# Fixed places on ScalarE for scaled output copies and rounding of operand sums, and a second pass that begins with one block product alone

## The chip, the cores and the metric

The kernel runs on one core of a Trainium2 chip. The metric is the device time of one execution in microseconds; the time of a kernel is the median of its runs.

## The reference

One layer of a hybrid decoder trunk for a sequence of 1024 tokens and 1024 channels, in float32: two token mixers in parallel, then an MLP.

```
h = rms_norm(x); xa, ga, q, f, v, g, m_a, m_b = split(h @ w_in)      # eight times 1024 columns
xa = causal_conv4(xa)
r, i = sigmoid(xa @ w_r + b_r), sigmoid(xa @ w_i + b_i)              # blocks of 256 channels
a = exp(-8 r softplus(-lam)); y_a = scan(a, sqrt(1 - a^2) i xa) * gelu(ga)
qf, f_gate, kf = silu(q), lb + (1 - lb) sigmoid(f), (1 - lb) sigmoid(-f)   # 8 heads of 128
o[t] = qf[t] . S[t];  S[t] = f_gate[t] S[t-1] + kf[t] v[t]           # linear attention with decay
y_b = rms_norm(o) * hg_norm * silu(g)
x = x + (sigmoid(m_a) y_a + sigmoid(m_b) y_b) @ w_out
x = x + relu(rms_norm(x) @ w_up)^2 @ w_down;  out = rms_norm(x)
```

## The kernel before

**Products.** Every float32 product is made of three matmuls (`mm3`, L132 to L134). Both operands are split into a rounded high part and the rest: ScalarE (ACT) casts the high part (L87, names ending in H), VectorE (DVE) subtracts to get the low part (L88, names ending in L). The 1024 tokens are two halves of T = 512, c = 0 and 1; the normalised, transposed input lies in `hT`, as hT00, hT01 (first half) and hT10, hT11.

**First pass.** Eight stages i, for each half c four pairs p of 128-channel heads. A stage projects xa, q, f and v for its 256 channels, gates xa by `rg_lru` (TensorE (PE) makes the products pr and pi, ACT their sigmoids rw and ri, then exponentials rr and rw for the recurrence), and runs the linear attention `hgrn` of the stage before in between: the driver calls `hgrn(i)` with a function that advances stage i + 1 by so many steps, and `GO` says how many steps come ahead of each block of hgrn's matmuls. A step is mostly six matmuls of 128x512. The blocks are sc (scores: of 32 columns, then sc32 at L633 and sc64 at L644), pk (transposes of kk), pkv, po (the output, whose squares ACT sums at L712). POOL makes the reciprocal root `hrs` (L720), and eight ACT instructions (L724) write the scaled output `on`; a stage later `on_T` transposes it (poT, L386), and onT goes to memory. The four PSUM banks of tag "pj" serve projections, pr, pi and v; "hg" has two banks (among others po, poT and the transposes xT), "sc" two.

In the stages of the first half the rows of the second half of the tokens are loaded, normalised and transposed too (x10 to x13): transposes xT, ACT's copy hT1xH, DVE's hT1xL.

In the four stages of the second half and after them, `make_combos` prepares operands of the second pass: for each of eight pieces POOL makes eight sums r (L309 to L316); ACT casts four of them (L323: t1 and n2 into stt, T3 and T4 into stT), POOL subtracts (L326), and SP stores them. `combos_on(n)` advances this by n half pieces.

**Order.** The matmuls of the first pass are pinned in the order in which they are written (`pinned`), and `tc.keep_in_program_order` pins others, such as splits and the t1 casts; a scheduler puts the rest where it finds room, by priority. What an engine has in its order it runs in that order, and it stops at an instruction whose operand isn't ready.

**Second pass.** The gates g, mb of the last pair are projected by `last_stage`. Then 14 quads of blocks (`own`) are multiplied by a scheme of seven block products (`gate_step`, steps 0 to 6) in place of eight; a step is twelve matmuls of 128x512. Steps 0 and 3 use the input directly, 1 uses t1, 2 n2, 4 T3, 6 T4. Quads come as q340 and q341, q350 and q351, and so on; ACT and DVE split blocks of them (wA..., "a" and "d") and sums of blocks (ws..., "sums", "b" and "c"). The first two quads and the four operands are loaded on SP's queue in an order written out with `in_turn`.

## Time and profile before

| | |
|---|---|
| time, median of 3 runs | 1644.56 us (1638.29 to 1646.38) |
| profiled execution, its own time | 1646.05 us |
| its span, first to last instruction | 1644.3 us |
| mean granted TensorE clock | 0.979 |
| PE busy | 1549.7 us, 94% |
| DVE busy | 1218.3 us, 74% |
| ACT busy | 819.9 us, 50% |
| POOL busy | 190.6 us, 12% |

The first pass reaches from the start to about 630 us, the second pass with its gates and the output product to about 960 us, and the norm and the MLP from there to the end. The times of a timeline are us from the start of the span; in its rows stand start, duration, engine, line, operation and tile, and in brackets how long the engine was idle before and what ended that. A granted clock of 1.00 is full speed.

### The profile page before, as it was taken

The page shows a single profiled execution, that of the slowest core. Times are in us where ns is not written, and L with a number is a line of the kernel's source. Part 1 is how long each engine was busy: PE and PEld are TensorE (multiplying, and loading weights), DVE is VectorE, ACT ScalarE, POOL GpSimd, SP SyncE. Part 2 cuts the span into 40 slices and gives each one's busy share as a digit, 9 for nine tenths or more (in the row PEclk, how much of TensorE's full clock was granted, in tenths as well). Part 3 has the DMA queues.
Part 4 walks back from the last instruction along what each step waited for, and adds up shares of the span by engine and source line. Part 5 has one row for each costly group of instructions (what it writes and reads, how often), then busy time and mean ns, then how long its engine had stood idle before and what let it go on. Part 6 is the DMA issues. An engine that isn't in the chain of part 4 may idle for free.

```text
span 1644.3 us, 23134 instructions
## 1 busy us (share of the span) xinstructions
PE 1549.7 (94%) x9072; PEld 1287.7 (78%) x9072; DVE 1218.3 (74%) x1706; ACT 819.9 (50%) x1341; POOL 190.6 (12%) x187
## 2 busy tenths in 40 slices
PE   7999889998898988999999997999999999999998
PEld 6877678887786776788888876788888878888886
DVE  5797565775969562878676469888788898878887
ACT  5646637465464632545444356676777642112213
POOL 1131101213746450000000000000000000000000
PEclk9999989999999999999999998999999999999999
DMA  6223122231424236433234783466666665666652
GB/s 234 90 91 109 60 83 72 92 130 69 135 90 136 71 116 257 165 115 128 90 137 157 294 278 132 172 253 255 261 236 244 241 267 208 245 262 260 252 222 103
DMA packets 72205, 280.07 MB, mean 170 GB/s; under 512 B 7712, under 2 KB 16032, under 8 KB 59168
## 3 DMA queue, kind: packets, MB, share of 16 engines
q1 hardware_dynamic: 69072, 267.58, 43.5%
q10 hardware_dynamic: 3024, 11.01, 1.8%
q8 instruction: 71, 1.16, 0.3%
q14 instruction: 38, 0.31, 0.1%
HBM read 193.63 MB, written 84.93 MB: 169 GB/s over the span
## 4 chain that ended last, share of the span: by engine, by line
PE 70%; DVE 13%; ACT 6%; POOL 5%; issue 4%; DMA 2%; ACTq 0%; DVEq 0%; POOLq 0%; SPq 0%
PE dX L132 3%; PE dX L133 3%; PE dX L134 3%; PE uX L132 3%; PE uX L134 3%; PE uX L133 3%; PE gX L133 3%; PE gX L132 3%; PE gX L134 3%; PE dY L134 2%; PE dY L133 2%; PE dY L132 2%; PE uY L134 2%; PE uY L132 2%; PE uY L133 2%
## 5 line engine op out<-in xcount | busy, mean ns | idle before, releaser
L88 DVE TENSOR_TENSOR wL<-raw,wH 128x1024 fp32r<-128x1024 f32 x100 | 123.7, 1240 | 104.2 <-ACT wH L87 102.4
L87 ACT CAST wH<-raw 128x1024 fp32r<-128x1024 f32 x100 | 104.9, 1049 | 75.3 <-PE po L133 36.6
L1360 DVE TENSOR_TENSOR acc<-acc,dX 128x512 f32<-128x512 f32 x128 | 85.0, 683 | 29.4 <-PE dX L134 28.4
L87 ACT CAST wA<-q 128x512 fp32r<-128x512 f32 x46 | 28.4, 621 | 132.4 <-PE dX L134 101.4
L1360 DVE TENSOR_TENSOR acc<-acc,dY 128x512 f32<-128x512 f32 x64 | 43.3, 685 | 15.6 <-PE dY L134 14.5
L155 POOL TENSOR_TENSOR rstd_h<-rstd_h,mhalf 128x1 f32<-128x1 f32 x8 | 5.5, 684 | 396.0 <-DVE rstd_h L154 396.0
L133 PE MATMUL po<-wL,y 128*128 128x512 f32 x128 | 50.0, 391 | 0.0
L134 PE MATMUL po<-wH,y 128*128 128x512 f32 x128 | 50.0, 390 | 0.0
L132 PE MATMUL po<-wH,y 128*128 128x512 f32 x128 | 49.8, 389 | 0.0
L1220 ACT ACTIVATE b<-b 128x512 f32<-128x512 f32 x48 | 30.2, 630 | 35.9 <-DVE b L1219 35.9
L326 POOL TENSOR_TENSOR stt<-r,stt 128x256 fp32r<-128x256 f32 x16 | 35.3, 2211 | 90.6 <-ACT stt L323 90.6
L88 DVE TENSOR_TENSOR wA<-q,wA 128x512 fp32r<-128x512 f32 x46 | 31.4, 685 | 14.4 <-ACT wA L87 14.4
L712 ACT ACTIVATE on<-po 128x128 f32<-128x128 f32 x64 | 16.8, 276 | 48.4 <-PE po L708 48.4
L413 DVE SCALAR_TENSOR_TENSOR xc<-xp,pvt,xc 128x512 f32<-128x512 f32 x48 | 40.4, 862 | 0.0
L906 DVE TENSOR_TENSOR s<-q,q 128x512 f32<-128x512 f32 x46 | 31.8, 693 | 1.5 <-DMA q<-mlp_in 1.0
L718 DVE TENSOR_SCALAR hssq<-hssq 128x8 f32<-128x8 f32 x8 | 1.4, 172 | 41.3 <-ACT on L712 41.3
L911 DVE TENSOR_TENSOR s<-q 128x512 f32<-128x512 f32 x46 | 31.6, 686 | 0.4
L1221 ACT ACTIVATE b<-b 128x512 f32<-128x512 f32 x48 | 30.0, 630 | 1.1
L323 ACT CAST stt<-r 128x256 fp32r<-128x256 f32 x16 | 6.4, 403 | 47.6 <-POOL r L315 47.5
L618 POOL TENSOR_SCALAR scT<-dd 32x256 f32<-32x256 f32 x32 | 21.1, 659 | 65.1 <-DVE dd L534 63.6
L133 PEld LDWEIGHTS po<-wL,y 128*128 128x128 f32 x128 | 24.0, 188 | 5.0
L134 PEld LDWEIGHTS po<-wH,y 128*128 128x128 f32 x128 | 24.0, 188 | 4.9
(2528 smaller groups left out, 5521.3 us busy)
## 6 DMA issues: line engine op xcount, KB each, us to landing
raw<-wts_in SPq DMA_DIRECT2D x96, 512.0 KB, 3.4
q<-mlp_in SPq DMA_DIRECT2D x92, 512.0 KB, 3.5
y<-yd SPq DMA_DIRECT2D x7, 1024.0 KB, 8.4
x<-x_in SPq DMA_DIRECT2D x8, 512.0 KB, 5.9
hd<-ri SPq DMA_DIRECT2D x16, 256.0 KB, 2.8
od<-onT ACTq DMA_DIRECT2D x8, 512.0 KB, 2.6
cdT<-stT SPq DMA_DIRECT2D x16, 256.0 KB, 3.1
o<-od SPq DMA_DIRECT2D x4, 1024.0 KB, 5.8
```

The source lines that it names most:

```text
L87: keep(A.copy(h, src))
L88: keep(V.tensor_tensor(out=lo, in0=src, in1=h.bitcast(F32), op=ALU.subtract))
L132: pin(PE.matmul(o, ah, bh, start=first, stop=False, **how))
L133: pin(PE.matmul(o, ah, bl, start=False, stop=False, **how))
L134: pin(PE.matmul(o, al, bh, start=False, stop=last, **how))
L326: G.tensor_tensor(out=lo, in0=src, in1=h.bitcast(F32), op=ALU.subtract)
L413: V.scalar_tensor_tensor(xc[:, s, :], xp[:, j : j + T], pvt[:, PV_CW + 8 * j + u : PV_CW + 8 * j + u + 1], xc[:, s, :], op0=ALU.mult, op1= ...
L906: V.tensor_tensor(out=sa[:, 0, :], in0=a21, in1=a22, op=ALU.add)
L911: V.tensor_tensor(out=sb[:, 0, :], in0=a21, in1=a11, op=ALU.add)
L1220: A.activation(b[:, at, :], b[:, at, :], AF.Relu, scale=-1.0 if at == 2 else 1.0)
L1221: A.activation(b[:, at, :], b[:, at, :], AF.Square)
L1360: V.tensor_tensor(out=dst, in0=dst, in1=banks[bk, pr], op=op)
```

## The change

- `GO` moves a step: two steps instead of one stand ahead of pk, and one instead of two ahead of po. All stages but the second do five steps of the f projection ahead of `rg_lru` instead of four, and their weight tiles are loaded in that order.
- The scaled copies of L724 are put into a function, `normalised`, that is called after `rg_lru` of the next stage and is pinned there; in the last stage after the first mb.
- All four casts of a half piece are pinned, not t1's alone, and the half pieces that were advanced after `rg_lru` are advanced ahead of it.
- The transposes x11 to x13 run at high priority (400).
- In the last stage smb takes another buffer, and the store of the second half of g2 comes behind `on_T`.
- The second pass makes steps 0, 3, 1, 2 of the first quad, with step 0 of the second quad behind them, in place of steps 0 and 3 of both; its loads are issued as q350, t1, n2, q351, T3, T4; the splits of its first blocks have high priority (600), and two pools change places.

```diff
-GO = (26, 5, 1, 1, 2)
+GO = (26, 5, 2, 1, 1)
...
-        at = {1: (0, 1, 2, 3, 4, 6, 5)}.get(i, range(7))
+        at = (0, 1, 2, 3, 4, 6, 5)
...
-            ins = A.copy(h, src)
-            if o == "t1":
-                tc.keep_in_program_order(ins)
+            tc.keep_in_program_order(A.copy(h, src))
...
-        for s, _ in both:
-            for n in range(4):
-                j = 4 * s + n
-                A.activation(on[:, j, :], po[s][:, n * P : (n + 1) * P], AF.Identity, scale=rs[:, j : j + 1])
+
+        def normalised():
+            for s, _ in both:
+                for n in range(4):
+                    j = 4 * s + n
+                    at = po[s][:, n * P : (n + 1) * P]
+                    ins = A.activation(on[:, j, :], at, AF.Identity, scale=rs[:, j : j + 1])
+                    tc.keep_in_program_order(ins)
+
+        got["normalised"] = normalised
...
-                transposed(xn1[n], hT[1], n, f"x1{n}")
+                with tc.high_priority(400):
+                    transposed(xn1[n], hT[1], n, f"x1{n}")
...
-        for _ in range(4 if i != 1 else 7):
+        for _ in range(5 if i != 1 else 7):
             next(fs)
             yield
+        if i > 3:
+            combos_on(1 if i == 4 else 2)
...
         yield from rg_lru(c, p, got, *got["xc"])
+        if i > 0:
+            gots[i - 1]["normalised"]()
         for n in ((0,), (1,), (2, 3))[i] if i < 3 else ():
             xn1[n] = next_rows(n)
-        if i > 3:
-            combos_on(1 if i == 4 else 2)
...
-            t = mt("tmp", f"smb{c}", (P, 2, T))
+            t = mt("ri", f"smb{c}", (P, 2, T))
...
-            nc.scalar.dma_start(g2d[:, 2 * c : 2 * c + 2, :], g)
             if c == 0:
+                nc.scalar.dma_start(g2d[:, 0:2, :], g)
+                gots[-1]["normalised"]()
                 yield
         on_T(NC - 1, NPAIR - 1, gots[-1])
+        nc.scalar.dma_start(g2d[:, 2:4, :], g2[1])
...
-    for o in ("t1", "n2", "T3", "T4"):
+    for o in ("t1", "n2"):
+        load_combo(o)
+    in_turn(raw_q[GQ + own[1]][1], mlp[GQ + own[1], 1])
+    for o in ("T3", "T4"):
         load_combo(o)
     pinned[0] = True
     for step in (0, 3):
-        for q in own[:2]:
-            gate_step(q, step)
+        gate_step(own[0], step)
     pinned[0] = False
...
-        for step in (0, 1, 2, 3, 4, 5, 6):
...
+        for step in (1, 2, 4, 5, 6) if q == own[0] else (0, 1, 2, 3, 4, 5, 6):
+            if q == own[1] and step == 0:
                 continue
+            pinned[0] = q < own[2]
             gate_step(q, step)
-            if q == own[0]:
...
+            if q == own[0] and step == 2:
+                gate_step(own[1], 0)
+            pinned[0] = False
```

The order of ACT in stage 7 of the first pass (c = 1, p = 3), from the squares of the attention before it to the f sigmoids; on12, po14 and po15 belong to that attention, rw13, pr16 and pr17 to the stage's gates. Before:

```order
L712 ACTIVATE on12_5192,hssq12_5193<-po15_5259 128x128 x4
L87 CAST wH70_5303<-raw70_5301 128x1024
L724 ACTIVATE on12_5192<-po14_5258,hrs12_5285 128x128 x4
L724 ACTIVATE on12_5192<-po15_5259,hrs12_5285 128x128 x4
L436 ACTIVATE rw13_5307<-pr16_5311,pvt_77 128x512
L436 ACTIVATE ri13_5308<-pi16_5312,pvt_77 128x512
L436 ACTIVATE rw13_5307<-pr17_5327,pvt_77 128x512
```

And with the change:

```order
L710 ACTIVATE on12_5192,hssq12_5193<-po15_5259 128x128 x4
L87 CAST wH70_5295<-raw70_5293 128x1024
L323 CAST stt15_5305<-r5_4990 128x256 x2
L323 CAST stT35_5312<-r5_4990 128x256 x2
L434 ACTIVATE rw13_5334<-pr16_5338,pvt_77 128x512
L434 ACTIVATE ri13_5335<-pi16_5339,pvt_77 128x512
L434 ACTIVATE rw13_5334<-pr17_5354,pvt_77 128x512
L87 CAST wH71_5330<-raw71_5328 128x1024
L434 ACTIVATE ri13_5335<-pi17_5355,pvt_77 128x512
...
L434 ACTIVATE rw13_5334<-rw13_5334,par_123 128x512 x2
L725 ACTIVATE on12_5192<-po14_5258,hrs12_5285 128x128 x4
...
L493 ACTIVATE f13_5404<-pj_f13_0_5206 128x512
```

The scaled copies moved from ahead of the first rw to ahead of the f sigmoids, and four casts of a piece's sums stand where they were.

The order of ACT earlier in that stage, around the copies kk and qf (L611 and L612, L609 and L610 with the change) that sc64 needs, from the convolution's first product on; r4 and r5 are the sums of pieces 4 and 5. Before:

```order
L397 ACTIVATE xc13_4936<-pj_xa13_1_4875,pvt_77 128x512
L323 CAST stt14_4976<-r4_4661 128x256
L323 CAST stT34_4983<-r4_4661 128x256 x2
L323 CAST stt15_5351<-r5_4990 128x256
L611 COPY kk12_4701<-kc12_4726 128x16x32
L612 COPY qf12_5096<-qb12_4718 128x16x32
L87 CAST wH68_5125<-raw68_5123 128x1024
```

And with the change:

```order
L395 ACTIVATE xc13_4936<-pj_xa13_1_4875,pvt_77 128x512
L323 CAST stt14_4976<-r4_4615 128x256 x2
L323 CAST stT34_4983<-r4_4615 128x256 x2
L609 COPY kk12_4701<-kc12_4726 128x16x32
L610 COPY qf12_5096<-qb12_4718 128x16x32
L87 CAST wH68_5125<-raw68_5123 128x1024
```

The cast of r5 that stood ahead of kk has moved to the place shown above.

The order of DVE in stage 3 (c = 0, p = 2 of the recurrence), where the low parts of the transposes x12 and x13 are made. Before, behind the recurrence's scans:

```order
L505 TENSOR_TENSOR qb02_1939<-qb02_1939,seg02_1932 128x32x2x8
L468 SCALAR_TENSOR_TENSOR ri02_1832<-a02_1834,hcar_126,ri02_1832 128x512
L88 TENSOR_TENSOR hT10L_89<-xT_x12_0_2005,hT10H_88 128x4x128
L88 TENSOR_TENSOR hT11L_87<-xT_x12_1_2012,hT11H_86 128x4x128
L505 TENSOR_TENSOR seg02_1932<-seg02_1932 128x32 x5
...
L88 TENSOR_TENSOR hT10L_89<-xT_x13_0_2085,hT10H_88 128x4x128
```

And with the change:

```order
L456 TENSOR_SCALAR rw02_1835<-rw02_1835 128x1024
L457 SCALAR_TENSOR_TENSOR a02_1838<-rr02_1837,rw02_1835 128x1024
L458 TENSOR_SCALAR a02_1838<-a02_1838 128x1024
L88 TENSOR_TENSOR hT10L_89<-xT_x12_0_2005,hT10H_88 128x4x128
L495 TENSOR_SCALAR f02_1921<-f02_1921,par_123 128x512
L88 TENSOR_TENSOR hT11L_87<-xT_x12_1_2012,hT11H_86 128x4x128
```

The low parts of x12 stand now ahead of the f chain, directly behind the recurrence's coefficients, where the scans were twenty rows later.

The order of ACT at the end of the first pass, with the splits of the first quads (q340, q350). Before:

```order
L832 ACTIVATE smb1_6065<-mb10_6015 128x512
L832 ACTIVATE smb1_6065<-mb11_6016 128x512
L834 DMA g2d_105<-g21_5892 128x1024
L387 ACTIVATE onT13_6070<-poT130_6071,pvt_77 128x512
L387 ACTIVATE onT13_6070<-poT131_6077,pvt_77 128x512
L388 DMA od3_100<-onT13_6070 128x1024
L87 CAST wA1134_6115<-q340_6111 128x512
```

And with the change:

```order
L87 CAST ws134H_6173<-s340_6118 128x1024
L87 CAST wA1134_6115<-q340_6111 128x512
L87 CAST wA1135_6131<-q350_6128 128x512
L839 ACTIVATE smb1_6065<-mb10_6015 128x512
L87 CAST ws334H_6177<-s341_6119 128x1024
L839 ACTIVATE smb1_6065<-mb11_6016 128x512
L385 ACTIVATE onT13_6069<-poT130_6070,pvt_77 128x512
```

The splits of the first quad moved from behind onT to ahead of smb1.

## The prediction

> **What bounds the kernel now.** I read the page first, then the stretches, then what TensorE (PE) waits for, and last the places of those waits in the timeline.

> ```profile
> span 1644.3 us, 23134 instructions
> PE 1549.7 (94%) x9072; PEld 1287.7 (78%) x9072; DVE 1218.3 (74%) x1706; ACT 819.9 (50%) x1341; POOL 190.6 (12%) x187
> PE 70%; DVE 13%; ACT 6%; POOL 5%; issue 4%; DMA 2%; ACTq 0%; DVEq 0%; POOLq 0%; SPq 0%
> ...
> 100.00:700.00 600.00, 540.65 (x4388) 457.61 (x4382) 407.79 (x622) 318.43 (x632) 167.56 (x156) 0.95 0.31 112
> 700.00:960.00 260.00, 260.00 (x1149) 215.36 (x1148) 176.90 (x183) 111.94 (x145) 0.00 (x0) 1.00 0.43 158
> 960.00:1045.00 85.00, 70.36 (x322) 55.92 (x321) 69.21 (x98) 55.21 (x90) 5.47 (x8) 0.94 0.48 171
> 1045.00:1640.00 595.00, 590.15 (x2587) 483.87 (x2585) 489.70 (x669) 275.81 (x392) 0.00 (x0) 1.00 0.61 237
> ```

> The last four rows are stretches: length, busy us of PE, PEld, DVE, ACT, POOL, then the granted clock and DMA. PE is the bound. From 700 to 960 it never idles, and from 1045 on hardly. The change touches 100 to 700: there PE idles 600 − 540.65 = 59.4 us and has a mean clock of 0.95, which also costs time. The chain agrees: its 13% DVE, 6% ACT and 5% POOL are detours from a saturated PE. Nothing can be won outside this stretch, since the change keeps every matmul.

> PE's waits (us in total, times, longest) say who is late:

> ```profile
> PE poT L386 <- DVE hT10L L88: 12.4, 1, 12.4
> PE pr L132 <- ACT rw L436: 11.3, 6, 1.9
> PE sc L644 <- ACT qf L612: 7.5, 3, 2.7
> PE sc L633 <- DVE qb L505: 5.1, 3, 3.9
> PE gX L132 <- ACT wA L87: 3.8, 1, 3.8
> PE xT_x L162 <- ACT onT L387: 3.4, 1, 3.4
> PE pk L670 <- DVE dd L534: 2.6, 1, 2.6
> PE pk L670 <- DVE kk L505: 2.3, 2, 1.9
> PE gY L132 <- ACT ws334H L87: 1.0, 1, 1.0
> ```

> They sum to 49.4 of the 59.4 us. Waits for a late weight split in the two-channel projections, 5 us more, I leave in place.

> **The clock.** These PE rows (start, duration, idle before in brackets) stand around one pr wait, followed by two stretches after other waits:

> ```profile
> 326.77 0.39 PE L132 MATMUL pi<-xcH,wH 128*128 128x512 f32 x1
> 327.90 0.39 PE L134 MATMUL pi<-xcH,wL 128*128 128x512 f32 x1
> 330.13 0.50 PE L132 MATMUL pr<-xcH,wH 128*128 128x512 f32 x1 [1.84 <-ACT rw L436]
> 331.26 0.63 PE L132 MATMUL pr<-xcH,wH 128*128 128x512 f32 x1
> 204.20:217.90 13.70, 5.23 (x25) 5.23 (x26) 9.96 (x23) 1.62 (x3) 0.76 (x2) 0.50 0.20 77
> 450.00:456.80 6.80, 5.80 (x28) 4.73 (x29) 6.03 (x12) 6.74 (x10) 3.24 (x5) 0.50 0.37 116
> ```

> A wait of 1.84 us was followed by matmuls of 0.63 instead of 0.39 us, and the clock was 0.50 around the poT and sc waits. Five starts from 326.77 to 327.90 put one 128x512 product at 0.226 us, so a step of six at 1.36. The lost clock of the stretch is (1 − 0.95) × 600 = 30 us; part of it falls on idle time (in the two rows PE is busy 11.0 of 20.5 us), so 16 to 27 us of work are lost; I take 22. [...]

> **The change, term by term.** ACT around a pr wait, and a later cast in the same stages:

> ```profile
> 467.35 1.05 ACT L87 CAST wH<-raw 128x1024 fp32r<-128x1024 f32 x1
> 469.37 2.17 ACT L724 ACTIVATE on<-po,hrs 128x128 f32<-128x128 f32 x8 [0.96 <-POOL hrs L720]
> 471.38 0.74 ACT L436 ACTIVATE rw<-pr,pvt 128x512 f32<-128x512 f32 x1
> 449.51 0.40 ACT L323 CAST stt<-r 128x256 fp32r<-128x256 f32 x1 [11.54 <-POOL r L315]
> 449.82 0.61 ACT L611 COPY kk<-kc 128x512 f32<-128x512 f32 x1
> ```

> (a) *Scaled copies after tanh.* The gate's first sigmoid waits behind 0.96 us for POOL and the eight copies, 3.1 us in all; the second pr needs that bank, and waits 1.9 us. With the copies gone from there (four casts of 0.40 come instead in the four later stages, about 1.4 us), the six waits go: −11.3 (ends −5 and −11.3). The price: ACT's f sigmoids come behind the copies, 2.17 us, and in later stages one weight cast of 1.05, less the 1.9 that is no longer waited, so 1.3 us later. The four PE banks of projections are held longer: a v tile can then wait for f's bank, 0.6 us in six stages, +3.6 (ends 0 and +9, seven times 1.3).

> (b) *Next-half transposes at high priority.*

> ```profile
> 195.95 0.69 DVE L460 TENSOR_SCALAR a<-a 128x1024 f32<-128x1024 f32 x1
> 211.90 0.71 DVE L88 TENSOR_TENSOR hT10L<-xT_x,hT10H 128x512 fp32r<-128x512 f32 x1
> ```

> hT10L now comes directly behind the first row, some 15 us earlier than the second, so the 12.4 us wait ends. Next late are the second row's transposes, behind ACT's copies and the scaled `on` (2.17), so I leave 3 us: −9.4 (ends −6, −12.4). DVE carries the same work; wL for the next two tiles moves ahead of qb there, and if ACT's wH is late, qb waits behind it, covered by the 15 us just freed.

> (c) *Rounding in fixed places.* DVE in a stage without POOL work and in one with it, then POOL's first and last of eight sums, then what DVE waits for:

> ```profile
> 276.78 0.68 DVE L460 TENSOR_SCALAR a<-a 128x1024 f32<-128x1024 f32 x1
> 277.38 1.21 DVE L88 TENSOR_TENSOR wL<-raw,wH 128x1024 fp32r<-128x1024 f32 x1
> 411.07 1.75 DVE L88 TENSOR_TENSOR wL<-raw,wH 128x1024 fp32r<-128x1024 f32 x1
> 412.74 1.23 DVE L460 TENSOR_SCALAR a<-a 128x1024 f32<-128x1024 f32 x1
> 413.49 1.07 POOL L309 TENSOR_TENSOR r<-hT00H,hT00L 128x256 f32<-128x256 f32 x1
> 421.65 1.07 POOL L316 TENSOR_TENSOR r<-r 128x256 f32<-128x256 f32 x1
> DVE hssq L718 <- ACT on L712: 41.3, 7, 6.3
> ```

> The eight sums take 9.2 us, and 0.5 us is added to each of about ten DVE instructions that build qa, qb and kc: 5 us in the chain that releases the sc products. They start about 10 us sooner now, partly where DVE waits for ACT's squares (last row). Also the cast that held ACT 11.54 us ahead of the kk and qf copies is gone, about 1 us. Against this stand f 1.3 us later and PE 1.9 earlier: net about 2 to 3 us a stage, in four stages. Of the 7.5 + 5.1 = 12.6 us I take −8 (ends 0, −12.6).

> (d) *GO and five f steps.* One more step of 1.36 us ahead of pk shortens three pk waits, 4.9 in all, by −3 (ends −1.5, −4.9); the step taken from ahead of po is covered by kv waits under 1 us. The x10 transposes waiting for onT gain −1.5 (ends 0, −3.4).

> (e) *Second pass.*

> ```profile
> SPq L953 <- DVE wA L88: 29.6, 1, 29.6
> 633.54 1.14 ACT L87 CAST wA<-q 128x512 fp32r<-128x512 f32 x2 [0.40 <-ACT onT L387]
> ```

> The operand split that gX waits for, cast at 633.54 behind onT, now stands ahead of the second smb on ACT; the ws sums too. Of 3.8 + 1.0 I take −4.5 (ends −2, −4.8). On SP, t1 and n2 no longer queue behind q351 (the 29.6 us); T3, T4, g2 and q360 do. Cover: five block products (twelve 128x512 matmuls each, 2.7 us) run before T3 is used, 13.6 us, so q351's hold costs nothing; were it as long as before, T3 would come late and PE wait about as long as it did for wA, 3.8. The pool swap and the merged casts cost nothing: no instruction on PE depends on them.

> (f) *Clock.* PE is busy 5.23 us in poT's stretch, so 2.6 are lost there; behind gX and behind about three of the six pr waits I count half of the 6.80 above, 3.4 us with 1.7 lost, four times: 6.8. Of the 22 us I take these, −9 (ends −4, −20); the stretches behind sc stay, since a wait stays there.

> Sum: −11.3 + 3.6 − 9.4 − 8 − 3 − 1.5 − 4.5 − 9 = −43.1. The profiled execution took 1646.05 us, 1.5 above the median of the runs, 1644.56: about 1603. The weak ends: −5 + 9 − 6 + 0 − 1.5 + 0 − 2 − 4 = −9.5; the strong ones −69.4. All weak ends together are unlikely; half way from the sum to them is −26, to the strong −56.

> **Rivals.** *R1, DVE stays the bound in the four later stages.* The slowed instructions follow POOL wherever it runs, and DVE is 407.79 us busy in these 600. Then (c) is 0, and four of the six pr waits only move to sc: −11.3 + 7.6 + 3.6 − 9.4 − 3 − 1.5 − 4.5 − 5 (clock) = −23.5, 1622. For it speaks 0.68 → 1.23; against, the 6.3-us wait into which the sums move. [...]

> *R2, everything goes.* The strong ends, with the 3.6 for the v tile and 4 us of clock left: −62, 1584. It needs the sc waits gone, and of POOL's two rounds of sums per later stage one stays where it is, beside the instructions that end just ahead of sc; kk here takes 1.22 us while a round runs to 378.8, against 0.7 for other 128x512 instructions such as hT10L:

> ```profile
> 374.67 1.22 DVE L505 TENSOR_TENSOR kk<-kc,seg 128x512 f32<-128x512 f32 x1
> 377.69 1.06 POOL L316 TENSOR_TENSOR r<-r 128x256 f32<-128x256 f32 x1
> ```

> *R3, slower: a pinned cast stops ACT.* All rounding casts now stand ahead of rw. If POOL's sum, or SP's store that frees the two-buffer stt, is late, ACT stops with pr banks full and PE with it; before, such a cast floated. Price as seen once, 11.54 us each; eight pieces. Five such stops turn −43 into +15: 1661. Decided by whether the sums end before ACT reaches the casts. Against: the cast that began at 449.51, as soon as its sum was there, now stands just ahead of the rw of 471.38, so its sum has 22 us to spare; the sums of the other round are read a round later in the same way.

> *R4, no net change.* f and the copies late in all seven stages: 2.17 + 1.05 us of ACT ahead of f plus 2 for a bank, 5.2 × 7 = 36: −7, 1639.

> **How the numbers follow.** My forecast (1592 to 1614) gets 0.50, R1 0.25, R2 0.11, R4 0.08, R3 0.06. About 0.5%, 8.2 us, is what a measurement can tell. Faster is forecast, R1 and R2, 0.86; same R4, 0.08; slower R3, 0.06. Range 1586 to 1630: below it half of R2, above it R3, R4 and a little of R1.

> **What would show it.** (a) No wait of pr for rw; f sigmoids behind L725. (b) hT10L near L458's row, no 12-us wait of poT. (c) L458 and the wL behind it at 0.7 and 1.2 us in the later stages. (e) No gX wait on wA. (f) Clock over 0.97 in the stretch before 700. The prediction is wrong if waits of sc for qb or qf sum to over 15 us, or ACT waits over 5 us for POOL r ahead of rw.

## The result and the profile after

The changed kernel takes 1585.17 us (median of 4 runs, 1584.78 to 1588.3), the kernel before 1644.82: a ratio of 0.9649, 95% interval 0.962 to 0.9677. That is faster by 60 us where 42 were forecast, and 0.8 us below the lower end of the range. The profiled execution took 1585.07 us. Of the four executions of one kernel below, undo_go, one took 3110.78 us and is left out; it is the profiled one, so that kernel's trace is not read. From the changed kernel's page: the span, the engines, the chain; then the stretch of the first pass's stages, which was 600 us long (PE busy 540.65, clock 0.95) and is 538 now.

```profile
span 1583.3 us, 23131 instructions
PE 1531.4 (97%) x9072; PEld 1278.8 (81%) x9072; DVE 1209.5 (76%) x1706; ACT 820.8 (52%) x1341; POOL 162.6 (10%) x187
PE 76%; DVE 13%; ACT 6%; issue 2%; DMA 2%; POOL 1%; DVEq 0%; SPq 0%; POOLq 0%; ACTq 0%
...
100.00:638.00 538.00, 521.15 (x4386) 447.63 (x4380) 400.40 (x628) 319.63 (x633) 148.03 (x157) 0.99 0.36 126
```

Span less PE's busy time is PE's idle time. Before it was 1644.3 − 1549.7 = 94.6 us, now 1583.3 − 1531.4 = 51.9. So 42.7 of the 61.0 us of span are waits that went; the other 18.3 are busy time, with the same matmuls (x9072). Most of that is the clock: PE was busy 48.75 us inside half-clock stretches (granted clock 0.50) before and 19.05 us now, and half of such time is counted as lost (at clock 0.50 the 128x512 matmuls started 0.43 us apart, before, 331.26 to 333.39 us, against 0.226 at full clock), so 24.4 and 9.5, a gain of 14.9. The remaining 3.4 us are not clock; 2.9 of them lie in the second pass, where matmuls follow each other faster now, without a gap that these views count as idle.

By place: the first pass, up to the end of the last poT, took 630.4 us and takes 580.4, a gain of 50.0 (36.1 idle, 13.3 clock). From there to the end of the last gX it was 277.6 and is 266.6, a gain of 11.0. The rest, which the change does not touch, is 736.3 in both.

The largest of PE's waits that are left in the part that the change touches, and ACT's wait for one of POOL's sums (us in total, times, longest):

```profile
PE sc L642 <- DVE qf L503: 4.7, 3, 1.6
PE po L703 <- DVE sn L689: 2.8, 1, 2.8
PE xT_x L162 <- ACT onT L385: 1.7, 1, 1.7
PE sc L631 <- DVE qb L503: 1.5, 3, 0.5
PE xT_x L162 <- ACT on L725: 1.4, 2, 0.9
PE sc L642 <- ACT scT L647: 1.4, 1, 1.4
PE poT L384 <- ACT on L725: 1.0, 2, 0.6
PE pk L668 <- DVE kk L503: 1.0, 1, 1.0
ACT stt L323 <- POOL r L313: 6.9, 1, 6.9
```

Of the rows of before, poT for hT10L (12.4), pr for rw (11.3), gX and gY (4.8) are gone altogether, and so are the waits of pj_xa and g for a weight. New are, among others, po's wait for sn, 2.8 us, and sc's for scT, 1.4. ACT and DVE at the places of the prediction, from the timeline:

```profile
435.18 1.05 ACT L87 CAST wH<-raw 128x1024 fp32r<-128x1024 f32 x1
436.14 0.71 ACT L323 CAST stt<-r 128x256 fp32r<-128x256 f32 x2
438.09 0.69 ACT L434 ACTIVATE rw<-pr,pvt 128x512 f32<-128x512 f32 x1 [0.62 <-PE pr L134]
440.81 0.69 ACT L434 ACTIVATE rw<-pr,pvt 128x512 f32<-128x512 f32 x1 [0.67 <-PE pr L134]
448.35 2.15 ACT L725 ACTIVATE on<-po,hrs 128x128 f32<-128x128 f32 x8
...
192.29 0.69 DVE L458 TENSOR_SCALAR a<-a 128x1024 f32<-128x1024 f32 x1
192.90 0.68 DVE L88 TENSOR_TENSOR hT10L<-xT_x,hT10H 128x512 fp32r<-128x512 f32 x1
```

ACT now waits for pr, no longer PE for ACT; the copies come ten us after the first rw. hT10L lies directly behind L458, 19 us earlier than before (211.90).

### The profile page after: what moved, and what is told of

Read it like the earlier page. It is cut to its first block, busy times and chain, and to the rows that moved or that the text cites. A ratio compares the mean times of both kernels' runs of the same rounds, so it can differ in the third digit from the quotient of the medians.

```text
span 1583.3 us, 23131 instructions
## 1 busy us (share of the span) xinstructions
PE 1531.4 (97%) x9072; PEld 1278.8 (81%) x9072; DVE 1209.5 (76%) x1706; ACT 820.8 (52%) x1341; POOL 162.6 (10%) x187
## 4 chain that ended last, share of the span: by engine, by line
PE 76%; DVE 13%; ACT 6%; issue 2%; DMA 2%; POOL 1%; DVEq 0%; SPq 0%; POOLq 0%; ACTq 0%
PE dX L132 3%; PE dX L133 3%; PE uX L132 3%; PE dX L134 3%; PE uX L134 3%; PE gX L134 3%; PE gX L133 3%; PE uX L133 3%; PE gX L132 3%; PE uY L134 2%; PE gY L134 2%; PE gY L133 2%; PE uY L132 2%; PE uY L133 2%; PE gY L132 2%
## 5 line engine op out<-in xcount | busy, mean ns | idle before, releaser
L88 DVE TENSOR_TENSOR wL<-raw,wH 128x1024 fp32r<-128x1024 f32 x100 | 124.3, 1245 | 91.4 <-ACT wH L87 89.9
L87 ACT CAST wH<-raw 128x1024 fp32r<-128x1024 f32 x100 | 105.0, 1050 | 71.2 <-PE po L133 36.6
L87 ACT CAST wA<-q 128x512 fp32r<-128x512 f32 x46 | 28.4, 621 | 132.6 <-PE dX L134 101.4
L134 PE MATMUL po<-wH,y 128*128 128x512 f32 x128 | 50.0, 391 | 0.0
L132 PE MATMUL po<-wH,y 128*128 128x512 f32 x128 | 49.8, 389 | 0.0
L411 DVE SCALAR_TENSOR_TENSOR xc<-xp,pvt,xc 128x512 f32<-128x512 f32 x48 | 40.4, 864 | 0.0
L88 DVE TENSOR_TENSOR wA<-q,wA 128x512 fp32r<-128x512 f32 x46 | 31.5, 686 | 10.3 <-ACT wA L87 10.3
L324 POOL TENSOR_TENSOR stt<-r,stt 128x256 fp32r<-128x256 f32 x16 | 23.2, 1467 | 93.1 <-ACT stt L323 93.1
L132 PEld LDWEIGHTS po<-wH,y 128*128 128x128 f32 x128 | 24.0, 188 | 5.0
L134 PEld LDWEIGHTS po<-wH,y 128*128 128x128 f32 x128 | 24.0, 188 | 4.9
L703 PE MATMUL po<-v,scT 128*128 128x128 f32 x128 | 24.7, 286 | 2.8 <-DVE sn L689 2.8
```

Source lines behind the costliest of these rows:

```text
L87: keep(A.copy(h, src))
L88: keep(V.tensor_tensor(out=lo, in0=src, in1=h.bitcast(F32), op=ALU.subtract))
L132: pin(PE.matmul(o, ah, bh, start=first, stop=False, **how))
L134: pin(PE.matmul(o, al, bh, start=False, stop=last, **how))
L411: V.scalar_tensor_tensor(xc[:, s, :], xp[:, j : j + T], pvt[:, PV_CW + 8 * j + u : PV_CW + 8 * j + u + 1], xc[:, s, :], op0=ALU.mult, op1= ...
L703: pin(PE.matmul(on_ps, scT[:, 4 * s + n, :], vn(s, n), start=True, stop=only))
```

## The experiments

All times of one execution are spans; idle is the span less PE's busy time. The median and the ratio to the kernel before, measured beside it on the same chip, decide. The ratios of undo_copies, undo_go, conv_late, sums_late and sums_late_last overlap with that of the changed kernel, so their differences from it are not clear of noise. Spans differ by chance too: the part behind the last gX, which no edit touches, takes 736.3 to 739.1 us in these traces.

| kernel | median us | ratio, 95% interval | span | PE idle | PE busy |
|---|---|---|---|---|---|
| before | 1644.82 | | 1644.3 | 94.6 | 1549.7 |
| changed | 1585.17 | 0.9649 (0.962 to 0.9677) | 1583.3 | 51.9 | 1531.4 |
| undo_copies | 1588.47 | 0.9652 (0.9633 to 0.9671) | 1587.0 | 57.6 | 1529.4 |
| undo_go | 1589.51 | 0.9663 (0.9636 to 0.969) | | | |
| undo_copies_go | 1607.73 | 0.9777 (0.9752 to 0.9803) | 1606.1 | 69.0 | 1537.1 |
| undo_rounding | 1608.85 | 0.9783 (0.9762 to 0.9804) | 1610.8 | 68.6 | 1542.2 |
| undo_transposes | 1603.17 | 0.9735 (0.9711 to 0.976) | 1602.4 | 64.5 | 1537.9 |
| undo_second | 1599.2 | 0.972 (0.9702 to 0.9738) | 1597.2 | 61.4 | 1535.8 |
| wait_4 | 1608.79 | 0.9788 (0.9757 to 0.9818) | 1604.9 | 68.0 | 1536.9 |
| conv_late | 1591.18 | 0.9671 (0.965 to 0.9692) | 1588.8 | 56.7 | 1532.1 |
| conv_later | 1598.29 | 0.9718 (0.9696 to 0.974) | 1596.1 | 59.2 | 1536.9 |
| conv_later_sums | 1606.09 | 0.9765 (0.9741 to 0.9789) | 1605.2 | 67.9 | 1537.3 |
| sums_late | 1580.79 | 0.9609 (0.9587 to 0.9631) | 1580.3 | 50.0 | 1530.3 |
| sums_late_last | 1582.61 | 0.9617 (0.9597 to 0.9637) | 1584.3 | 50.6 | 1533.7 |

### The copies back ahead of the sigmoids

```diff
-        def normalised(): ...          # called behind the next stage's rg_lru, pinned
+        for s, _ in both: ...          # the eight copies, as before, not pinned
```

> The changed kernel with the scaled copies put back ahead of the gate's sigmoids, not pinned; all else as changed (1585.2 us). Theory A (a wait costs itself and the half clock of its window): seven pr waits of 1.9 us or so come back, 11 to 13 us, and about half of them bring a half-clock stretch, 1.7 us each, some 6 more: 1601 to 1605. Theory B (in the four later stages DVE's chain is the bound and hides PE's waits): only the three pr waits of the first half cost, 6 us, and the sc waits of the later stages shrink by what pr waits: 1590 to 1593. [...]

Measured: 1588.47 us, 3.3 more than the changed kernel, with ratios that overlap; under both forecasts. PE's waits in it:

```profile
PE pr L132 <- ACT rw L434: 6.8, 6, 1.8
PE pk L668 <- DVE kk L503: 5.1, 4, 1.4
PE sc L642 <- DVE qf L503: 2.5, 3, 1.0
```

The six pr waits come back, but not with the 11.3 us of before: three in the first half are 0.5 us (at 181.64, 246.90 and 308.77) and three in the second 1.8. In the later stages they cost little: sc waits less (2.5 instead of 4.7 in all), pk more (5.1 instead of 1.0), and the three half-clock stretches behind sc are gone, with one behind a pr wait in their place, so that PE's lost clock is 6.9 instead of 9.5 us. Such a stage takes 65.3 to 67.1 us, where the changed kernel takes 65.0 to 65.1. So moving the copies was not what ended most of the pr wait. The fifth f step was the candidate: it gives ACT 1.36 us more before pr, and 1.9 less 1.36 is about 0.5.

### The steps back, alone and with the copies

```diff
-GO = (26, 5, 2, 1, 1)
+GO = (26, 5, 1, 1, 2)
...
-        for _ in range(5 if i != 1 else 7):
+        for _ in range(4 if i != 1 else 7):
```

> The changed kernel with GO = (26, 5, 1, 1, 2), four f steps ahead of rg_lru and the old order of the weight tiles. Theory A (the fifth step covers what the copies would have covered, so one of the two is enough for pr): pr's waits stay under 0.7 us, as the copies are still behind; pk waits 1 to 2 us in each later stage, 5 us more in all: 1588 to 1593. Theory B (the copies alone end pr's waits and the step is without worth): 1584 to 1587.

Measured: 1589.51 us, the median of three runs (1587.07 to 1591.92). The time is where theory A had it, 4.3 us above the changed kernel, but the intervals overlap (0.9636 to 0.969 against 0.962 to 0.9677), so theory B is not ruled out, and where PE waits in this kernel is not known.

> Both undone: scaled copies ahead of the gate's sigmoids, and the old GO and f steps. Theory A (either of the two ends most of the pr waits of the first half): the pr waits are again 1.9 us six times, 11 us, with half clock behind about half of them, so much more than the 3.3 us of the copies alone: 1597 to 1604. Theory B (the two add up): the 3.3 us of the copies and that of the step alone, under 1594.

Measured: 1607.73 us, 22.6 more than the changed kernel, where the two alone cost 3.3 and 4.3. That is beyond theory A's range, and theory B is out.

```profile
PE pr L132 <- ACT rw L434: 14.9, 6, 3.1
PE pk L668 <- DVE kk L503: 8.2, 3, 2.7
```

Three pr waits are 1.85 us again and three are 3.1, since four casts now stand there as well. So either edit covers most of what the other covers, and the prediction's term (a) belongs to both: taken out singly, each looks cheap. The steps were taken back as one, `GO`, the fifth f step and the order of the weight tiles; which of them covers pr was not tried apart. The po wait for sn is gone here and stays in undo_copies, so it comes with the steps.

### Rounding and half pieces back

```diff
-            tc.keep_in_program_order(A.copy(h, src))
+            ins = A.copy(h, src)
+            if o == "t1":
+                tc.keep_in_program_order(ins)
...
-        if i > 3:
-            combos_on(1 if i == 4 else 2)      # ahead of rg_lru
...
+        if i > 3:
+            combos_on(1 if i == 4 else 2)      # behind rg_lru
```

> The changed kernel with the casts of the sums unpinned (but t1's) and the half pieces advanced behind the gates again. Theory A: POOL's sums lie again beside the DVE instructions that build qa, qb and kc, about 5 us more in each of four chains, and a cast again stops ACT ahead of the kk and qf copies: sc waits rise from 6.2 us to 12 to 20, with the half clock behind them: 1595 to 1605. Theory B (the loss moves with the sums, wherever they are): sc waits within 3 us of now, 1583 to 1589.

Measured: 1608.85 us, 23.7 more: beyond theory A, and theory B is out. DVE's kb in the changed kernel and in this one, ACT's cast in this one, and waits of ACT and PE in this one:

```profile
455.50 0.68 DVE L503 TENSOR_TENSOR kb<-kk,f 128x512 f32<-128x512 f32 x1
...
468.57 1.22 DVE L505 TENSOR_TENSOR kb<-kk,f 128x512 f32<-128x512 f32 x1
428.28 0.40 ACT L323 CAST stt<-r 128x256 fp32r<-128x256 f32 x1 [10.66 <-POOL r L315]
ACT stt L323 <- POOL r L315: 36.5, 4, 10.8
PE sc L644 <- ACT qf L612: 7.2, 3, 2.4
PE sc L515 <- DVE qb L505: 4.2, 1, 4.2
PE pj_xa L132 <- ACT v L375: 4.0, 2, 2.0
PE pv L132 <- ACT kk L496: 3.1, 3, 1.0
```

Both halves of term (c) are there: DVE's instructions at 1.22 instead of 0.68 us beside the sums, and a cast that stops ACT for 10.66 us ahead of the kk copy. The sc waits are 12.7 us in all, inside theory A's 12 to 20. But the cost is not in sc alone. It also shows as pj_xa waiting for ACT's copy of v and as pv waiting for f's bank. Idle time is up by 16.7 us and busy time by 10.8, all of it clock. The pinned casts and the earlier place of the half pieces were taken back together, so this run does not say which of the two does how much.

### The transposes without priority

```diff
-                with tc.high_priority(400):
-                    transposed(xn1[n], hT[1], n, f"x1{n}")
+                transposed(xn1[n], hT[1], n, f"x1{n}")
```

> The changed kernel without the high priority for the transposes x11 to x13. Theory A: hT10L lands again behind the scans, the wait of poT for it is again 9 to 13 us with 3 to 5 us of half clock: 1596 to 1603. Theory B (that wait covers work that then waits elsewhere, so it is not worth its length): 1586 to 1592.

Measured: 1603.17 us, 18.0 more, at theory A's upper end. The wait and its reason:

```profile
PE poT L384 <- DVE hT10L L88: 14.3, 1, 14.3
210.38 0.67 DVE L88 TENSOR_TENSOR hT10L<-xT_x,hT10H 128x512 fp32r<-128x512 f32 x1
```

Idle time grows by 12.6 us, busy time by 6.5, of which 6.0 are clock: the wait of 14.3 us brings a half-clock stretch of 17.1 us with it.

### The last stage and the second pass as before

```diff
-            t = mt("ri", f"smb{c}", (P, 2, T))
+            t = mt("tmp", f"smb{c}", (P, 2, T))
...
-        gate_step(own[0], step)
+        for q in own[:2]:
+            gate_step(q, step)
...                                      # loads, order of steps and splits as before too
```

> The changed kernel with the last stage and the second pass as before (order of block products, loads, splits without high priority, smb's buffer, stores), the rest as changed. Theory A: the wait of gX for wA of 3.8 us, that of gY of 1.0, some small ones of 2 us and a half-clock stretch of 1.7 come back, and the 1.8 us of g for its weight: 1592 to 1596. Theory B (with the earlier end of the first pass the loads were in time anyway): 1585 to 1588.

Measured: 1599.2 us, 14.0 more, above theory A.

```profile
PE pk L668 <- DVE kk L503: 4.2, 4, 1.1
PE gX L132 <- ACT wA L87: 3.8, 1, 3.8
PE gY L132 <- ACT ws334H L87: 1.0, 1, 1.0
```

gX's and gY's waits are back to the tenth. The pk waits stand in stages that this edit does not touch. There the half-clock stretch behind sc is missing (PE busy 61.5 us from one stage's scores to the next's instead of 62.8, idle 3.3 instead of 2.2; the stage takes 64.8 instead of 65.1): PE, faster, comes to pk before DVE has kk. A half-clock stretch in front of a late engine is nearly free here. So the pk waits are no cost of this part, and the first pass as a whole ends 0.6 us earlier than in the changed kernel. The places of the matmuls say what costs. gX begins 3.8 us behind the last poT, in the changed kernel 0.2 ahead of its end. Its first twelve matmuls take 5.3 instead of 2.8 us at half clock. The next 200, up to 640 us, lose 5.3 us in small delays, while PE comes to one split after the other (ws334, ws135, wA, ws136) just before it is ready; about half of that is in no row of PE's waits. Together these are 11.8 us. The first pass gives 0.6 back, and 2.8 lie behind the last gX, where nothing was edited.

### A wait of known size

```diff
+            for _ in range(4 if s == 0 else 0):
+                on_act(w[:, s, :], pr, AF.Identity)
             on_act(w[:, s, :], pr, AF.Sigmoid, bias=pvt[:, PV_BR + u : PV_BR + u + 1])
```

> The changed kernel with four extra ACT copies of pr's bank (some 0.6 us each) ahead of the first sigmoid in each of the eight stages; they change no value. PE's second pr waits about 2 us for it, in eight stages, 14 to 17 us. Theory A (a wait of about 2 us brings a half-clock stretch of 3.4 us in about half of its places): clock in the stretch of the stages down from 0.99 to 0.97, with 1.7 us lost for each stretch, 6 to 10 us: 1603 to 1612. [...] If DVE's chain is what PE waits for in the later stages, the sc waits there do not shrink, since f comes later too.

Measured: 1608.79 us, 23.6 more.

```profile
PE pr L132 <- ACT rw L434: 13.7, 7, 2.0
```

The waits have the size that was wanted. The time lies in theory A's range, but by luck: only two of the seven waits are followed by half clock, and of the lost time 16.1 us are idleness and 5.5 busy time, of which just 2.4 are clock, where theory A had 6 to 10. The two that half clock followed were 1.9 us long, and all seven average 2.0. What decides is not the length of a wait alone, and the kernel with copies and steps undone shows what does. Two of its pr waits, and the windows of 3.41 us in which they lie (length, PE busy first; clock third from the end), on the grid that its half-clock stretches start on:

```profile
184.86 0.51 PE L132 MATMUL pr<-xcH,wH 128*128 128x512 f32 x1 [1.86 <-ACT rw L434]
388.08 0.50 PE L132 MATMUL pr<-xcH,wH 128*128 128x512 f32 x1 [3.13 <-ACT rw L434]
...
181.89:185.30 3.41, 1.55 (x7) 0.97 (x7) 0.56 (x1) 3.24 (x10) 0.14 (x1) 1.00 0.45 153
185.30:188.72 3.42, 3.42 (x10) 2.64 (x9) 0.00 (x0) 0.77 (x2) 0.00 (x0) 0.50 0.00 1
383.27:386.69 3.42, 1.68 (x8) 1.06 (x6) 1.12 (x1) 2.63 (x11) 0.84 (x2) 1.00 0.36 115
386.69:390.10 3.41, 2.02 (x9) 1.69 (x10) 0.00 (x0) 2.25 (x6) 3.33 (x5) 1.00 0.58 210
390.10:393.51 3.41, 3.41 (x17) 2.83 (x16) 1.52 (x2) 2.95 (x4) 3.33 (x5) 1.00 0.41 141
```

The wait of 1.86 us inside one window (busy 1.55 of 3.41) was followed by a window at clock 0.50. The one of 3.13 us that falls half into each of two (busy 1.68 and 2.02) was followed by full clock, 1.00.

### The convolution behind qf, and behind kk

```diff
+                if j == 0 and qf_mul:
+                    how = mybir.DependencyInfo(mybir.DependencyClass.NoSync, mybir.DependencyReason.DATA)
+                    tc.add_manual_dep(ins.ins, qf_mul[-1].ins.name, how, reason="conv")
```

These two try to remove what is left of the sc waits by DVE's order: the edge makes the convolution's first instruction follow the product that makes qf, or, in the second, the last one that makes kk. The second also calls the convolution later, behind q's projection, from the third stage on.

> The changed kernel with the convolution's DVE instructions (L411) put behind the product that makes qf, by an order edge alone. Six instructions of 0.9 to 1.1 us stand there ahead of kc, qb, kk and qf now. Theory A (DVE's chain to qf is what is left of the sc waits): the sc waits of 6.2 us and their three half-clock stretches go: 1576 to 1581. Theory D (kc waits for PE's block of scores, not for DVE's place, or xcL comes late for pr): 1583 to 1590.

> The changed kernel with the convolution behind the last product that makes kk, which pk needs, not only behind qf. Theory A (with only qf freed the wait moved to pk, three times 2.9 us; freeing kk too ends it): neither sc nor pk waits over 1 us in the later stages: 1576 to 1582. Rival (the wait moves on again, to pr, since the convolution's low part is now made just ahead of pr): PE waits for xcL at pr, 1 to 3 us in each of seven stages: 1588 to 1600.

Measured: 1591.18 and 1598.29 us, 6 and 13 above the changed kernel, and only the second clear of noise. Neither theory A's time nor theory D's came; the second lies in its rival's range. The largest new wait of the first, and that of the second:

```profile
PE pk L673 <- DVE kk L508: 8.5, 3, 2.9
PE po L709 <- DVE sn L695: 14.2, 6, 2.5
```

The sc waits for qb and qf in the later stages are gone in both, as theory A has it. But the convolution, 5 to 6 us of DVE, stands then ahead of kk, and in the second kernel ahead of the states sn that po needs, in the first half's stages too, which had no wait. There a stage takes 65.7 instead of 61.5 us; the later ones take 64.0 to 65.5. The rival named pr and xcL, and PE waits for xcL once, 1.2 us, so its time was met by luck. The wait moves.

### POOL's first round of sums later

```diff
-        if i > 4:
-            combos_on(2)                       # behind the convolution's first product
...
         got["q1"] = q_of(c, p, pq)
         yield
+        if i > 4:
+            combos_on(2)
```

> The changed kernel with the first of each later stage's two rounds of POOL sums (and its four casts) moved from behind the convolution's first product to behind the q sigmoids, so that no POOL work stands beside the DVE instructions that make kc, qb, kk and qf. Theory A (POOL beside DVE costs 0.5 us an instruction, wherever that is, and this is what is left of the sc waits): kk and qf take 0.7 instead of 1.2 us, the sc waits of 6.2 us shrink to 2 or less, no half-clock stretch behind them: 1574 to 1580. Rival (a pinned cast stops ACT, since the round's sums now end only just ahead of the next round's casts): ACT waits for POOL r ahead of rw, PE at pr, 1590 or more.

Measured: 1580.79 us, ratio 0.9609 (0.9587 to 0.9631) against 0.9649 (0.962 to 0.9677) of the changed kernel: the lowest median here, though the two intervals overlap by a little. kk in the changed kernel and in this one, and this one's waits:

```profile
417.50 1.21 DVE L503 TENSOR_TENSOR kk<-kc,seg 128x512 f32<-128x512 f32 x1
...
411.41 0.68 DVE L503 TENSOR_TENSOR kk<-kc,seg 128x512 f32<-128x512 f32 x1
PE pkv L678 <- ACT kT L673: 2.2, 4, 0.6
PE sc L631 <- DVE qb L503: 2.7, 1, 2.7
```

In the three stages concerned the time from the start of one stage's scores to the next's falls from 65.0 to 62.1 us, and PE idles 0.7 us in each. This is theory A, 9 us of stages, though its time is 0.8 above that range. Part is given back in the last stage, where a sc wait of 2.7 us for qb with half clock behind it is new, and some 2 us behind the last gX, where nothing was edited.

> Both: the convolution behind kk and the first round of sums behind the q sigmoids. If each does what its theory A says, the two take away the same waits, and the sum is little more than one of them: 1573 to 1580. If POOL's sums now run beside the convolution, which stands just ahead of pr, xcL comes late and pr waits: 1590 to 1605.

Measured: 1606.09 us.

```profile
PE po L709 <- DVE sn L695: 11.6, 7, 2.3
PE pr L132 <- ACT rw L439: 8.9, 3, 3.0
```

The convolution's new wait stays, and pr waits 3 us in three stages, for rw and not for xcL as the expectation had it; its time, 1590 to 1605, is passed by 1 us. Two edits for the same wait do not add up when one of them takes the place into which the other moves its work.

### The last stage's sums later

```diff
-        combos_on(2)                           # ahead of the first projection
...
             pp = yield from plain(c, w, "g")
+            if c == 0:
+                combos_on(2)
```

> The kernel sums_late (1580.8 us) with the last stage's round of casts and sums also moved, from ahead of its first projection to behind it; the casts of piece 7 now stand on ACT directly behind those of piece 6, ahead of the copies of the score blocks sc32 and sc64, with POOL's eight sums between them. Theory A (POOL's sums beside the chain to qb are the 2.7 us wait of sc that is left in that stage): that wait goes, 1576 to 1579. The prediction's rival R3 (a pinned cast that waits for POOL's sum stops ACT, and PE with it): ACT waits about 10 us for POOL r, the score copies come late, and PE waits 5 to 10 us at po or the banks of the next projections: 1584 to 1592.

Measured: 1582.61 us, no gain over sums_late (0.9597 to 0.9637 against 0.9587 to 0.9631), and between the two ranges.

```profile
546.01 0.40 ACT L323 CAST stt<-r 128x256 fp32r<-128x256 f32 x1 [5.59 <-POOL r L313]
549.02 0.36 ACT L647 COPY scT<-sc 32x256 f32<-32x256 f32 x1
PE pk L668 <- ACT scT L647: 5.1, 1, 5.1
```

The sc wait of 2.7 us is gone, and in its place the pinned cast stops ACT (5.59 and 2.18 us for two sums), the copy scT queues behind it, and PE waits 5.1 us. This is the prediction's rival R3 at one place.

## Why the prediction was right or wrong

The sign was right, and so was the kind of gain at each place that was named; the size was not. Against −43.1 us the span moved by −61.0. The time lies next to R2, which had 1584 us and a chance of 0.11, but by number only: R2 needs the sc waits gone, and 6.2 us of them are left.

- **(f) The clock was the largest miss:** −9 taken, −14.9 measured, within its bound (−20). The 22 us of lost clock ahead of 700 us were right (43.7 us of busy time in half-clock stretches). The prediction kept the stretches behind sc because a wait stays there. Before, the waits of 2.4 to 3.9 us held stretches of up to 6.83 us; now two waits of 0.5 and 1.6 us together bring one of 3.41, and the stretches went with waits that were only shortened. Part of this is the waits' place in time: in undo_second the same two waits bring none.
- **(a) The pr waits ended, −11.3 as said, but for another reason too.** The runs give the moved copies alone 3.3 us, the steps alone 4.3, both 22.6. The step at fault is that the fifth f step was priced under (d), at pk, and its 1.36 us of cover for pr was not counted. The +3.6 for a v tile that waits for f's bank did not come: no such wait is in the profile.
- **(b) −9.4 and x10's −1.5.** Of 12.4 + 3.4 us before, 1.4 + 1.7 + 1.0 are left at the transposes, −11.7 by the waits, as sized. The run without priority puts 18.0 us on it, since the wait carries clock with it.
- **(c) −8 for sc: 12.6 became 6.2, −6.4,** near to what was taken. But the term was priced on sc alone, and the runs put 23.7 us on this edit: late ACT also holds back v and f. The weight waits of pj_xa and g, 5.3 us, which the prediction left in place, went as well, and no run that takes one part back has them again; which parts ended them is open.
- **R1 was wrong in its premise.** The loss does not move with the sums unchanged. In the stage shown, the moved sums stand beside a pause of DVE of 5.6 us and then slow two instructions on it (ri 1.76 us and rw 1.13, where the first half's stages, without sums, have 1.22 and 0.69), and kb goes from 1.22 to 0.68 us. For the round that was not moved, the premise holds (kk at 1.21), and sums_late removes it.
- **(d)** pk went from 4.9 to 1.0, −3.9 against −3. But the step taken from ahead of po was not covered, as the prediction had it: po waits 2.8 us for sn.
- **(e) −4.5 was too small:** this stretch gained 11.0 us, 1.7 of them clock. gX and gY went by their 4.8, and most of the rest is small delays by late splits further on, which the prediction did not price. q351's place cost nothing, as said.
- **R3** came once, at a small price: in the last stage a pinned cast stopped ACT for 6.87 us, the copy scT queued behind it, and PE waited 1.4 us. Before, ACT waited four times for POOL's sums, 47.5 us in all. The last run shows R3 again, for 5.1 us of PE.

The parts taken back one by one cost 3.3 + 4.3 + 23.7 + 18.0 + 14.0 = 63.3 us; with copies and steps taken together, 78.3, against 60 for the whole. They overlap, and the first two are not clear of noise, so none of these is that part's share.

## What to carry to other kernels

Price a wait with the clock behind it: here 42.7 us less idleness brought 14.9 us of clock, some of it by waits that were only shortened. How much a single wait brought hung on where it fell in time: one of 1.86 us was followed by half clock, one of 3.13 was not. A part that undoes cheaply may only be covered by another part, so undo pairs that act on the same wait. And a helper engine's work that slows a neighbour (here kk took 1.21 us beside POOL's sums and 0.68 without) belongs where that neighbour waits; moving the neighbour's own work about only moved the wait here.

## What the runs showed of the hardware

POOL and DVE slowed each other in these runs; by what means they do not show. 128x512 products on DVE such as kk and kb took 1.21 to 1.22 us beside POOL's sums and 0.68 without. In the changed kernel POOL's sums took 0.74 us where DVE paused, and up to 1.72 where DVE worked on wL (443.07, 1.23 us) and ri (444.21, 1.76 us):

```profile
440.26 0.74 POOL L309 TENSOR_TENSOR r<-hT00H,hT00L 128x256 f32<-128x256 f32 x1
443.17 1.72 POOL L313 TENSOR_TENSOR r<-r 128x256 f32<-128x256 f32 x1
```

POOL's busy time in the kernel fell from 190.6 to 162.6 us, and to 142.4 in sums_late, with the same 187 instructions. It is no measure of what DVE loses, though: undo_rounding has 157.8.
